# Score products of a gated recurrence: full 128 x 128 matmuls against column groups of 32 and 64 in heads 1 to 7

## The chip, the core and the metric

The kernel runs on one core of one Trainium2 chip. The metric is the device time of one execution in microseconds (us), and less is better. Five engines run beside each other and wait for each other through semaphores: TensorE (PE; its weight loads are shown apart as PEld), VectorE (DVE), ScalarE (ACT), GpSimd (POOL) and SyncE (SP), which here only issues DMAs.

## What is computed

The reference is a trunk of two layers on 256 tokens of 1024 features in fp32: a gated linear recurrence (HGRN2, 8 heads of 128 features), a SwiGLU, block attention, a second SwiGLU, with a norm ahead of each. The change is in the recurrence:

```python
q, fz, inp, og = jnp.split(proj, [...], axis=-1)     # proj = h @ w_in
q = jax.nn.silu(q)
f = lbf + (1.0 - lbf) * jax.nn.sigmoid(fz)
k = 1.0 - f
...
cum = jnp.cumsum(gb, axis=2)                         # gb = log f, in chunks of 64 tokens
diff = cum[:, :, :, None, :] - cum[:, :, None, :, :]
decay = jnp.exp(jnp.where(causal[:, :, None], diff, -jnp.inf))
scores = jnp.einsum('bhtn,bhsn,bhtsn->bhts', qb, kb, decay)
o = (jnp.einsum('bhts,bhsd->bhtd', scores, ib)
     + jnp.einsum('bhtn,bhnd->bhtd', qb * jnp.exp(cum), state))
```

So a token t sees a token s at or before it, and the product of their query and key is weighted, feature by feature, with the product of all forget gates f from s + 1 to t.

## The kernel before

**Main stream.** TensorE works through one long list of weight pieces. For each head the function `feature_major` computes three projections (forget, query, output gate) from 8 pieces of 128 x 128 weights each. `mm_w` issues three matmuls of 256 columns for each piece: weights and activations are split into a high and a low part, and high x high, low x high and high x low are added. The high part of a weight (`whi`) is made by ACT (L471), the low part (`wlo`) by DVE (L473), in blocks of 1024 columns, from weights that SP's queue loads. That is 72 main matmuls a head, into banks of the PSUM ring `psB`.

**The scores of a head.** `Core.scores` does not run over chunks. It splits the 256 x 256 score matrix by the distance of the two tokens: level m (2, 4, 8, 16, 32, 64, and 128 as the last one) holds the pairs whose tokens lie in the two halves of one block of 2m tokens. For each level `Core.step` has DVE and ACT make keys and queries that carry the gates' products up to the middle of the block, so that one matmul of keys by queries gives the level's scores. One such matmul of 128 keys by 128 queries gives the pairs between all blocks, of which only those within a block are wanted. They lie near the diagonal: `take` (DVE, `copy_predicated` with a mask) copies them into the score matrix `pm`; for levels 32 and 64 and the last one `far` (ACT) copies the square parts. Only these products are fp32 and not split, and each is issued by the hardware program as two matmuls with a weight load each. Per head there are:

- `s0`: two products for level 2 (rows named `psA<-mov,k`), into bank `b0`
- `level` for m = 4, 8 and 16 into a second bank, and for m = 32 and 64 into `b3` (rows `psA<-q,k`; level 64 is `psA<-q,bt`, since its keys lie inside the tile `bt`)
- the sums of the diagonal, with a matrix of ones as the weights (`psA<-q,ones`), into `b0`
- the last level, `kk` x `q128`, into `b3` (`psA<-bt,k`)
- `values`, the score matrix by the values `ii`, into `b4` (`psA<-bt,ii`)

These four banks are new for each head from the PSUM ring `psA`, which has four.

**Order.** The program's order is set while the kernel is written out, by the class `Order`. It keeps a planned clock for each engine. Main matmuls are issued in their list's order, and each moves the plan's time on. All other work is queued with a planned cost and a due time (`od.op(engine, cost, ...)`); after every main matmul or two `pump` emits what is ready in the plan. An operation of TensorE is put between main matmuls as soon as its operands are planned to have been ready for 1500 ns. `ct(n)`, the planned cost of an fp32 product, is 216 ns for 128 queries. The planned costs move nothing on the chip by themselves, but they decide where in TensorE's list a product stands, and in what order DVE, ACT and POOL take their work.

Of the kernel before, what the change touches and what calls it, by code (L numbers as in the profile page):

```python
# [335 lines left out]
def hybrid_trunk(ctx: ExitStack, tc: tile.TileContext, wts, xT, par, gfin, tab, onehot, masks, out):  # L336
# [218 lines left out]
    def mm(o, a, b, start=False, stop=False):  # L555
        T.matmul(o, a, b, start=start, stop=stop, skip_group_check=True)  # L556
# [311 lines left out]
    def normed(h, b, due):  # L868
# [4 lines left out]
              alloc=[t], due=due)  # L873
        return t, lambda: t.tile

    class Core:


# [61 lines left out]
        def step(self, m, due):  # L940
            Q, K, tot = self.Q, self.K, self.tot[m]
            if m < 64:
                k, kn = self.k1 if m == 1 else K[2], K[2]
                n = P // m
                bc = lambda z: cut(tot, z, (n + 1 - 2 * z, 2), (2, n // 2), (0, m))
                if m == 1:

                    q, pair = self.mov, self.tot[2]
                    od.op("V", cv(P), lambda: V.tensor_tensor(
                        cut(q, 0, (385, 2), (64, 2), (2, 32)), cut(q, P, (192, 2), (1, 2), (2, 32)),  # L950
                        cut(tot, 0, (P + 1, 2), (2, 2), (4, 32)), op=OP.mult), reads=[q, tot], writes=[q], due=due)
                    od.op("V", cv(P), lambda: V.tensor_tensor(
                        cut(q, 1, (383, 2), (64, 2), (2, 32)), cut(q, 192, (64, 2), (1, 2), (2, 32)),
                        cut(pair, 0, (64, 2), (1, 2), (2, 32)), op=OP.mult), reads=[q, pair], writes=[q], due=due)
                    od.op("V", cv(P), lambda: V.tensor_tensor(
                        first(kn, 1), k[:, :P].rearrange("p (a t) -> p a t", a=2), second(tot, 1), op=OP.mult),
                        reads=[k, tot], writes=[kn], due=due)
                    return
                elif m == 2:
                    q, qn = self.mov, Q[4]  # L960
                    of = lambda z: cut(q, 64 * z, (448 - P * z, 2), (2, 32), (1, 2))
                else:
                    q, qn = Q[m], Q[2 * m]
                    of = lambda z: (first, second)[z](q, m)
                od.op("V", cv(P), lambda: V.tensor_tensor(second(qn, m), of(1), bc(0), op=OP.mult), reads=[q, tot],
                      alloc=[qn], due=due)
                o = od.op("A", ca(P), lambda: A.activation(first(qn, m), of(0), AF.Copy), reads=[q], writes=[qn],
                          due=due + .1)
                o.deps.append(qn.writers[0])

                kk, kn = self.kk, K[2 * m]
                if m == 2:
                    od.op("V", cv(P), lambda: V.tensor_tensor(first(kk, m), first(k, m), bc(1), op=OP.mult),
                          reads=[k, tot], alloc=[kk], due=due)
                    o = od.op("A", ca(P), lambda: A.activation(second(kk, m), second(k, m), AF.Copy), reads=[k],
                              writes=[kk], due=due + .1)
                    o.deps.append(kk.writers[0])
                else:
                    od.op("V", cv(P), lambda: V.tensor_tensor(first(kk, m), first(kk, m), bc(1), op=OP.mult),
                          reads=[kk, tot], writes=[kk], due=due)  # L980
                od.op("A", ca(P), lambda: A.activation(
                    joint(kn, 2 * m).rearrange("p (b z i) -> p b z i", z=2, i=2 * m),
                    cut(kk, 0, (4 * m, 32 // m), (P + 2 * m, 2), (1, 2 * m)), AF.Copy), reads=[kk], alloc=[kn], due=due + .2)
                return
            self.q128 = q = new("q128", [P, P], 2)
            Q, k = Q[64], self.kk

            def last():
                A.activation(q[:, :64], Q[:, P:192], AF.Copy, scale=tot[:, 3:4])
                A.activation(q[:, 64:], Q[:, 192:], AF.Copy)  # L990
                A.activation(k[:, :64], k[:, :64], AF.Copy, scale=tot[:, 1:2])
            od.op("A", 3 * ca(64) + 186, last, reads=[Q, k, tot], writes=[k], alloc=[q], due=due)

        def scores(self, due):
            h, Q, K, mov = self.h, self.Q, self.K, self.mov
            pm = pms[h % 2]
            moff = {m: 2 * P + P * i for i, m in enumerate(LEVELS)}

            def take(m, src):
                d = ((2 * m, 64 // m), (1, m))  # L1000
                V.copy_predicated(cut(pm, m, (S - m, 2), *d), cut(mk, moff[m], (64, 2), (m, 64 // m), (1, m)), src)

            def level(b, c, m):

                mm(b[:, c:c + P], joint(K[m], m), second(Q[m], m), start=True, stop=True)

            b0 = bank("A")
            ev = self.even

            def s0():  # L1010


                for a, (c, to) in enumerate(((64, 64), (S, 192))):
                    mm(b0[:, to:to + P].rearrange("p (y x) -> p y x", y=2), K[2][:, a * P:a * P + P],
                       cut(mov, c, (P, 2), (1, 64)), start=True, stop=True)
            od.op("T", 2 * ct(P), s0, reads=[K[2], mov], alloc=[b0], due=due)

            def s0e():
                v = b0[:, :384].rearrange("p (a y x) -> p a y x", a=2, y=3)[:, :, 0:3:2]
                V.copy_predicated(pm[:, 0:3:2].rearrange("p a (x z) -> p a z x", z=2),  # L1020
                                  mk[:, :2 * P].rearrange("p (a z x) -> p a z x", a=2, z=2), v)
            od.op("V", cv(P), lambda: take(2, cut(b0, 64, (192, 2), (2, 32), (1, 2))), reads=[b0, mk], writes=[pm], due=due)
            b, o1 = bank("A"), None
            for i, m in enumerate((4, 8, 16)):
                o = od.op("T", ct(P), lambda m=m, i=i: level(b, P * i, m), reads=[K[m], Q[m]], due=due,
                          **(dict(writes=[b]) if i else dict(alloc=[b])))
                o.deps += [o1] if i else []
                o1 = o
                od.op("V", cv(P), lambda m=m, i=i: take(m, cut(b, P * i, (64, 2), (m, 64 // m), (1, m))), reads=[b, mk],
                      writes=[pm], due=due)  # L1030
            od.op("T", ct(P), lambda: mm(cut(b0, 0, (320, 2), (1, 64)), ones128, ev[:, EVEN].rearrange("p (a x) -> p a x", a=2),
                                         start=True, stop=True), reads=[ev], writes=[b0], due=due)
            od.op("V", cv(S), s0e, reads=[b0, mk], writes=[pm], due=due)
            b3, o1 = bank("A"), None
            for i, m in enumerate((32, 64)):
                o = od.op("T", ct(P), lambda m=m, i=i: level(b3, P * i, m), reads=[K[m], Q[m]], due=due,
                          **(dict(writes=[b3]) if i else dict(alloc=[b3])))
                o.deps += [o1] if i else []
                o1 = o
            o3 = od.op("T", ct(P), lambda: mm(b3[:, 2 * P:3 * P], self.kk[:, :P], self.q128.tile, start=True, stop=True),  # L1040
                       reads=[self.kk, self.q128], writes=[b3], due=due)
            o3.deps.append(o1)

            def far():
                for r, n, a, t, c in ((0, 32, 0, 32, 0), (64, 32, 0, 96, 32), (32, 32, 2, 0, 64), (96, 32, 2, 64, 96),
                                      (0, 64, 0, 64, P), (64, 64, 2, 0, 192)):
                    A.activation(pm[r:r + n, a, t:t + n], b3[r:r + n, c:c + n], AF.Copy)
                A.activation(pm[:, 1, :], b3[:, 2 * P:3 * P], AF.Copy)
            od.op("A", 1500, far, reads=[b3], writes=[pm], due=due)

            b4 = bank("A")
            hs = slice(h * P, h * P + P)

            def values():
                mm(b4[:, :S], ii[:, 0, hs], pm[:, 0:2, :].rearrange("p a t -> p (a t)"), start=True)
                mm(b4[:, P:S], ii[:, 1, hs], pm[:, 2, :], stop=True)
            od.op("T", ct(S) + ct(P), values, reads=[ii, pm], alloc=[b4], due=due)
            self.b4 = b4
# [22 lines left out]
    for h in range(NH):  # L1081
# [6 lines left out]
        if h == 0:  # L1088
            for k in range(KT):
                x0[k].free()  # L1090
    for k in range(KT):
        xs[k].free()
    sto.finish("A", 40)
# [577 lines left out]
```

## Time and profile before

| | |
|---|---|
| runs of the kernel | median 604.89 us of 3 (604.63 to 607.67) |
| the profiled execution | 605.56 us |
| its span, first to last instruction | 603.8 us |
| clock that TensorE was granted | 0.998 of full speed |
| TensorE's weight loads, whole program | 566.9 us busy |
| DMA | 120.85 MB, mean 200 GB/s |

The span is what the trace's rows add up to; the 1.8 us around it are start and end of the execution. In rows of groups, `out<-in` are the tiles by their names, `128*128 128x256` the rows and columns of the weights and the shape of what is streamed, `x64` the number of instructions, then their busy time in all and the mean duration of one. TensorE's matmuls are pipelined: their durations overlap, and how much of its time one takes is seen from when the next one starts. Timelines give start and duration in us from the span's beginning.

The recurrence of the eight heads lies between some 36 and 126 us, with 11 us a head.

### The profile page before, as it was taken

To read this page: it belongs to the slowest core of one execution; us is meant where nothing else is said; L and a number is where in the kernel's file an instruction comes from. 1 tells how busy PE (TensorE), PEld (TensorE's weight loads), DVE (VectorE), ACT (ScalarE), POOL (GpSimd) and SP (SyncE) were. 2 spreads that over 40 slices of the span, in tenths; PEclk is the share of its full clock that TensorE was granted. 3 is DMA by queue.
4 is the path that set the end of the run, shared out by engine and by line. 5 is a ranking of instruction groups with operands and counts; after the bars stand their busy time and mean duration, and the time that the engine had idled before them with its cause. 6 is when DMAs were issued, how large, how long until landed. Compare 5 with 4: busy or idle time off the path is not lost.

```text
span 603.8 us, 12020 instructions
## 1 busy us (share of the span) xinstructions
PE 595.6 (99%) x4508; PEld 566.9 (94%) x4508; DVE 514.7 (85%) x938; ACT 414.5 (69%) x816; POOL 62.4 (10%) x109
## 2 busy tenths in 40 slices
PE   9999999999999999999999999999999999999995
PEld 7899999999999999999988899999999999999984
DVE  6799988869797889889999678876789798889985
ACT  7698998957676476666838576655676576667763
POOL 0034141100101111110000100000100000000003
PEclk9999999999999999999999999999999999999999
DMA  8845542554847989889645764437565677778601
GB/s 315 327 167 190 178 166 95 170 170 161 261 152 158 270 232 254 258 249 263 236 164 170 254 208 153 163 140 236 177 213 164 223 239 232 227 215 256 196 34 69
DMA packets 35558, 120.85 MB, mean 200 GB/s; under 512 B 4812, under 2 KB 6348, under 8 KB 35501
## 3 DMA queue, kind: packets, MB, share of 16 engines
q1 hardware_dynamic: 31484, 109.05, 52.0%
q0 software_dynamic: 3056, 10.29, 10.1%
q10 hardware_dynamic: 960, 0.76, 0.4%
q8 instruction: 35, 0.57, 0.4%
q14 instruction: 23, 0.18, 0.1%
HBM read 118.71 MB, written 1.38 MB: 199 GB/s over the span
## 4 chain that ended last, share of the span: by engine, by line
PE 97%; DVE 1%; issue 0%; ACT 0%; POOL 0%; DVEq 0%; POOLq 0%; ACTq 0%
PE psB L556 50%; PE psA L556 47%; DVE ii L1318 1%; PE psB L1477 0%; PE psB L1381 0%; PE psA L1525 0%; DVE raw L1556 0%; DVE wlo L473 0%; PE psA L735 0%; PE psB L735 0%; DVE raw L1595 0%; DVE hl L1267 0%; DVE u L1257 0%; ACT fa L1579 0%; POOL ident masks.py:199 0%
## 5 line engine op out<-in xcount | busy, mean ns | idle before, releaser
L473 DVE TENSOR_TENSOR wlo<-raw,whi 128x1024 fp32r<-128x1024 f32 (+1 forms) x186 | 220.2, 1200 | 26.7 <-ACT whi L471 26.2
L471 ACT ACTIVATE whi<-raw 128x1024 fp32r<-128x1024 f32 (+1 forms) x185 | 188.2, 1038 | 43.7 <-PE psA L556 24.4
L556 PE MATMUL psB<-xh,whi 128*128 128x256 f32 x608 | 171.7, 286 | 0.0
L556 PE MATMUL psB<-xh,wlo 128*128 128x256 f32 x608 | 166.8, 278 | 0.0
L556 PE MATMUL psB<-xl,whi 128*128 128x256 f32 x608 | 162.3, 278 | 0.0
L556 PE MATMUL psA<-xh,whi 128*128 128x256 f32 x544 | 151.2, 281 | 0.0
L556 PE MATMUL psA<-xh,wlo 128*128 128x256 f32 x544 | 148.8, 277 | 0.0
L556 PE MATMUL psA<-xl,whi 128*128 128x256 f32 x544 | 143.7, 277 | 0.0
L556 PEld LDWEIGHTS psB<-xh,wlo 128*128 128x128 f32 x608 | 114.5, 188 | 0.7
L556 PEld LDWEIGHTS psB<-xh,whi 128*128 128x128 f32 x608 | 114.4, 188 | 0.7
L556 PEld LDWEIGHTS psB<-xl,whi 128*128 128x128 f32 x608 | 111.6, 189 | 0.0
L556 PEld LDWEIGHTS psA<-xh,wlo 128*128 128x128 f32 x544 | 102.4, 188 | 0.7
L556 PEld LDWEIGHTS psA<-xh,whi 128*128 128x128 f32 x544 | 102.2, 188 | 0.9
L556 PEld LDWEIGHTS psA<-xl,whi 128*128 128x128 f32 x544 | 99.2, 188 | 0.0
L1245 ACT ACTIVATE sgq<-sgq 128x256 f32<-128x256 f32 x44 | 18.2, 415 | 24.8 <-DVE sgq L1243 24.8
L556 PE MATMUL psB<-whi,hl 128*128 128x512 f32 (+1 forms) x91 | 35.1, 386 | 0.0
L556 PE MATMUL psB<-wlo,hh 128*128 128x512 f32 (+1 forms) x91 | 34.9, 383 | 0.0
L556 PE MATMUL psB<-whi,hh 128*128 128x512 f32 (+1 forms) x91 | 34.6, 380 | 0.1
L512 POOL DMA_DIRECT2D raw<-in_w_dram x13 | 11.7, 897 | 191.6 <-DVE wsum L504 177.8
L556 PE MATMUL psA<-whi,hh 128*128 128x512 f32 (+1 forms) x75 | 28.4, 379 | 0.3 <-DVE ii L1318 0.3
L556 PE MATMUL psA<-whi,hl 128*128 128x512 f32 (+1 forms) x75 | 28.6, 381 | 0.0
L556 PE MATMUL psA<-wlo,hh 128*128 128x512 f32 (+1 forms) x75 | 28.5, 380 | 0.0
(244 smaller groups left out, 980.7 us busy)
## 6 DMA issues: line engine op xcount, KB each, us to landing
raw<-in_w_dram SPq DMA_DIRECT2D x178, 512.0 KB, 4.3
bt<-in_w_dram SPq DMA_DIRECT2D x15, 512.0 KB, 5.1
raw<-in_w_dram POOLq DMA_DIRECT2D x13, 512.0 KB, 5.7
ii<-in_w_dram SPq DMA_DIRECT2D x9, 512.0 KB, 4.3
hT<-in_x_dram SPq DMA_DIRECT2D x8, 128.0 KB, 5.1
raw<-in_w_dram SPq DMA_DIRECT2D x4, 256.0 KB, 3.9
bt<-scr POOLq DMA_DIRECT2D x16, 64.0 KB, 6.6
bt<-in_w_dram POOLq DMA_DIRECT2D x2, 512.0 KB, 6.3
```

The costliest lines, as they stand in the source:

```text
L471: oa = od.op("A", ca(n), lambda h=h, r=src, o=o, n=n: A.activation(h[:, :n], r[:, o:o + n], AF.Copy), reads=[src], alloc=[h], due=due)
L473: ov = od.op("V", cv(n), lambda h=h, lo=lo, r=src, o=o, n=n: V.tensor_tensor(lo[:, :n], r[:, o:o + n], h[:, :n].bitcast(FT), op=OP.subtrac ...
L512: od.op("G", 1000, lambda: nc.gpsimd.dma_start(b.tile, wts[c0 // CHUNK], accum_op=OP.add), writes=[b], nbytes=2 * 524288, due=due + 1)
L556: T.matmul(o, a, b, start=start, stop=stop, skip_group_check=True)
L1245: od.op("A", ca(S), lambda: A.activation(s.tile, s.tile, AF.Silu), reads=[s], writes=[s], due=due)
L1318: V.scalar_tensor_tensor(at(), m[:, :], c[:, tt:tt + 1], at(), op0=OP.mult, op1=OP.add)
```

## The change

For heads 1 to 7, each of the score products named above, but for the last level's, is computed in pieces that hold the wanted blocks. The 128 keys of a product are cut into 4 groups of 32 weight columns, and each group is multiplied by the 32 queries that belong to it, and placed by `tile_position` in a column group of the array of its own, with its output in 32 partitions of the bank. Level 64 has two groups of 64 keys with 64 queries. What lies outside these blocks isn't computed; the masks and square copies don't use it. Head 0 still computes full products, which writes all of the banks once, and it takes the four banks of `psA` for good: `score_bank` hands heads 1 to 7 the same bank for the same use. The planned cost of a changed product is 80 ns instead of 216. The first product of the keys of a head (`kn` for m = 1) gets a dependency on the first writer of that tile.

```diff
+    def score_bank(h, i):
+        if h == 0:
+            b = bank("A", held=True)
+            r = Ring(lambda: b.tile, 1)
+            user = Buf(r)
+            user.readers, user.writers = b.readers, b.writers
+            r.past.append(user)
+            scored[i] = b, r, user
+            return b
+        b, r, _ = scored[i]
+        u = r.new()
+        scored[i] = b, r, u
+        return u
...
                         first(kn, 1), k[:, :P].rearrange("p (a t) -> p a t", a=2), second(tot, 1), op=OP.mult),
-                        reads=[k, tot], writes=[kn], due=due)
+                        reads=[k, tot], writes=[kn], due=due).deps.append(kn.writers[0])
...
+            cost = ct(P) if h == 0 else 80
+
             def level(b, c, m):
 
-                mm(b[:, c:c + P], joint(K[m], m), second(Q[m], m), start=True, stop=True)
-
-            b0 = bank("A")
+                keys, d = joint(K[m], m), ((m, 16 // m), (1, m)) if m <= 16 else ()
+                if h == 0:
+                    mm(b[:, c:c + P], keys, second(Q[m], m), start=True, stop=True)
+                elif m == 64:
+                    for z in range(2):
+                        small(b[64 * z:64 * z + 64, c + 64 * z:c + 64 * z + 64], keys, Q[m][:, 64 + 64 * z:P + 64 * z], z, 64)
+                else:
+                    for g in range(4):
+                        z, j, p = g % 2, g // 2, b[32 * g:32 * g + 32, :]
+                        if m == 32:
+                            at, to = m + 96 * z + 64 * j, c + 64 * z + 32 * j
+                            small(p[:, to:to + m], keys, Q[m][:, at:at + m], g, m)
+                        else:
+                            small(cut(p, c + 16 * g, (64, 2), *d), keys, cut(Q[m], m + 32 * g, (P - m, 2), (2 * m, 16 // m), (1, m)),
+                                  g, 32)
+
+            def small(o, keys, moving, g, n):
+                T.matmul(o, keys[:, n * g:n * g + n], moving, start=True, stop=True, skip_group_check=True,
+                         tile_position=(0, n * g))
+
+            b0 = score_bank(h, 0)
...
+                    if h:
+                        for g in range(4):
+                            small(cut(b0[32 * g:32 * g + 32, :], to + 16 * g, (64, 2), (1, 16)), K[2][:, a * P:a * P + P],
+                                  cut(mov, c + 16 * g, (P, 2), (1, 16)), g, 32)
+                        continue
...
-            od.op("T", 2 * ct(P), s0, reads=[K[2], mov], alloc=[b0], due=due)
+            od.op("T", 2 * cost, s0, reads=[K[2], mov], alloc=[b0], due=due)
...
+                for g in range(4):
+                    small(cut(b0[32 * g:32 * g + 32, :], 16 * g, (320, 2), (1, 16)), ones128,
+                          cut(ev, EVEN.start + 16 * g, (64, 2), (1, 16)), g, 32)
```

With another planned cost, products and main matmuls interleave in another way. Two places on TensorE show it. The first is around the `values` of head 0 (`psA<-bt,ii`); the `q` rows are head 1's levels, the `mov` row is level 2 of head 2. Before:

```order
L556 MATMUL psB<-xl_486,whi 128x256
L556 MATMUL psA<-q_839,k_826 128x128
L556 MATMUL psB<-xh_474,whi 128x256
L556 MATMUL psB<-xh_474,wlo 128x256
L556 MATMUL psB<-xl_496,whi 128x256
L556 MATMUL psA<-bt,ii 128x256
L556 MATMUL psA<-bt,ii 128x128
L556 MATMUL psA<-q_884,bt 128x128
L556 MATMUL psA<-mov,k_835 128x128 x2
L556 MATMUL psB<-xh_519,whi 128x256
```

and after the change, where a row of L1041 is a run of narrow matmuls:

```order
L556 MATMUL psB<-xl_419,whi 128x256
L1041 MATMUL psA<-mov,k_846 32x2x16 x8
L556 MATMUL psA<-bt,ii 128x256
L556 MATMUL psA<-bt,ii 128x128
L1041 MATMUL psA<-q_874,k_867 32x32 x4
L556 MATMUL psB<-xh_424,whi 128x256
L556 MATMUL psB<-xh_424,wlo 128x256
L556 MATMUL psB<-xl_437,whi 128x256
L556 MATMUL psB<-xh_426,whi 128x256
L556 MATMUL psB<-xh_426,wlo 128x256
L556 MATMUL psB<-xl_439,whi 128x256
L1041 MATMUL psA<-q_843,k_833 32x2x16 x4
```

Level 2 of head 2 has moved ahead of `values`, level 32 of head 1 (`32x32`) stands right behind it, and full matmuls lie between the three runs of narrow ones. The second place is TensorE at head 1's first level. Before, the last level's product of head 0 (`psA<-bt,k`) and level 8 of head 1 stand together:

```order
L556 MATMUL psB<-xl_496,whi 128x256
L556 MATMUL psA<-bt,k_572 128x128
L556 MATMUL psA<-q_802,k_788 128x128
L556 MATMUL psB<-xh_519,whi 128x256
L556 MATMUL psB<-xh_519,wlo 128x256
```

and after:

```order
L556 MATMUL psB<-xl_541,whi 128x256
L556 MATMUL psA<-bt,k_572 128x128
L1041 MATMUL psA<-q_766,k_760 32x2x16 x4
L1041 MATMUL psA<-q_692,ones_109 32x2x16 x4
L556 MATMUL psB<-xh_400,whi 128x256
```

Here level 4 and the diagonal's sums of head 1 have come together behind that product, so that two changed products share one place. In all, the 49 rows of L1041 stand in 44 places: between two places lies at least one full matmul, or, in one case, a change from groups of 32 to groups of 64.

More of the change, by code (lines that the diff above doesn't have):

```diff
@@ L874, in normed @@
         return t, lambda: t.tile
+    scored = {}
+    def score_bank(h, i):
[11 more added lines that the diff above has]
+        return u
     class Core:
@@ L1022, in scores @@
             od.op("V", cv(P), lambda: take(2, cut(b0, 64, (192, 2), (2, 32), (1, 2))), reads=[b0, mk], writes=[pm], due=due)
-            b, o1 = bank("A"), None
+            b, o1 = score_bank(h, 1), None
             for i, m in enumerate((4, 8, 16)):
-                o = od.op("T", ct(P), lambda m=m, i=i: level(b, P * i, m), reads=[K[m], Q[m]], due=due,
+                o = od.op("T", cost, lambda m=m, i=i: level(b, P * i, m), reads=[K[m], Q[m]], due=due,
                           **(dict(writes=[b]) if i else dict(alloc=[b])))
@@ L1030, in scores, with sums @@
                       writes=[pm], due=due)
-            od.op("T", ct(P), lambda: mm(cut(b0, 0, (320, 2), (1, 64)), ones128, ev[:, EVEN].rearrange("p (a x) -> p a x", a=2),
-                                         start=True, stop=True), reads=[ev], writes=[b0], due=due)
+            def sums():
+                if h == 0:
+                    mm(cut(b0, 0, (320, 2), (1, 64)), ones128, ev[:, EVEN].rearrange("p (a x) -> p a x", a=2),
+                       start=True, stop=True)
+                    return
+                for g in range(4):
+                    small(cut(b0[32 * g:32 * g + 32, :], 16 * g, (320, 2), (1, 16)), ones128,
+                          cut(ev, EVEN.start + 16 * g, (64, 2), (1, 16)), g, 32)
+            od.op("T", cost, sums, reads=[ev], writes=[b0], due=due)
             od.op("V", cv(S), s0e, reads=[b0, mk], writes=[pm], due=due)
-            b3, o1 = bank("A"), None
+            b3, o1 = score_bank(h, 2), None
             for i, m in enumerate((32, 64)):
-                o = od.op("T", ct(P), lambda m=m, i=i: level(b3, P * i, m), reads=[K[m], Q[m]], due=due,
+                o = od.op("T", cost, lambda m=m, i=i: level(b3, P * i, m), reads=[K[m], Q[m]], due=due,
                           **(dict(writes=[b3]) if i else dict(alloc=[b3])))
@@ L1049, in scores @@
             od.op("A", 1500, far, reads=[b3], writes=[pm], due=due)
-            b4 = bank("A")
+            b4 = score_bank(h, 3)
             hs = slice(h * P, h * P + P)
@@ L1090, in hybrid_trunk @@
                 x0[k].free()
+    for b, _, u in scored.values():
+        b.readers += u.readers + u.writers
+        b.held = False
     for k in range(KT):
```

## The prediction

> **What bounds the kernel now.** I read the page first: the busy shares, then the chain that ended last.
>
> ```profile
> span 603.8 us, 12020 instructions
> PE 595.6 (99%) x4508; PEld 566.9 (94%) x4508; DVE 514.7 (85%) x938; ACT 414.5 (69%) x816; POOL 62.4 (10%) x109
> PE 97%; DVE 1%; issue 0%; ACT 0%; POOL 0%; DVEq 0%; POOLq 0%; ACTq 0%
> ```
>
> The chain is TensorE (PE) for 97% of the span. A busy PE can still hide waiting, so the next view is that of the waits, for PE alone and the whole program. It has two rows:
>
> ```profile
> PE psA L556 <- POOL ident masks.py:199: 1.4, 1, 1.4
> PE psA L556 <- DVE ii L1318: 0.3, 1, 0.3
> ```
>
> PE waits once at the start and once in the last layer, never in the recurrence. So each microsecond that the change adds to or takes from PE's stream there should reach the end, as long as the other engines keep up. For that I read the table of windows over heads 1 to 7 (44 to 124 us; columns: stretch, length, then the busy time of PE, PEld, DVE, ACT, POOL, granted clock, DMA share, GB/s):
>
> ```profile
> 44.00:124.00 80.00, 80.00 (x686) 79.63 (x684) 72.95 (x186) 70.52 (x233) 20.20 (x48) 1.00 0.47 164
> ```
>
> PE is full and its clock is whole. VectorE (DVE) is busy for 72.95 of 80 us: about 7 us is the most that PE could gain here before DVE were the bound. If PE gets longer, nobody else is touched.
>
> **What is removed.** The groups of instructions, kept apart by shape, show the score products as fp32 matmuls of 128 x 128 with 128 queries. Each product is issued as two matmuls (two halves), each with its own weight load.
>
> ```profile
> L556 PE MATMUL psA<-q,k 128*128 128x128 f32 x64 | 11.8, 274 | 0.0
> L556 PE MATMUL psA<-mov,k 128*128 128x128 f32 x32 | 4.9, 274 | 0.0
> L556 PE MATMUL psA<-q,ones 128*128 128x128 f32 x16 | 3.1, 273 | 0.0
> L556 PE MATMUL psA<-q,bt 128*128 128x128 f32 x16 | 3.1, 273 | 0.0
> ```
>
> The counts are for eight heads: 128 halves, 64 products, 8 a head (levels 4, 8, 16, 32; two for level 2; the sums; level 64). Heads 1 to 7 lose 56 products. The 274 ns are a pipelined duration, not a price; the price is read from the chain, where a product stands between pieces of the main stream:
>
> ```profile
> 47.48 0.22 PE psA L556 x2
> 47.70 1.42 PE psB L556 x12
> ```
>
> A product takes 0.22 us of PE's time, 0.11 us a half; a main matmul takes 1.42/12 = 0.118 us. Removed: 56 x 0.22 = **12.3 us**.
>
> **What the narrow products cost in themselves.** Each of 49 products becomes 4 narrow ones (32 weight columns, 32 queries), hence 8 halves; each of the 7 of level 64 becomes 2 of 64, hence 4 halves. No row of this trace has a load of 32 columns or two column groups at once, so I bound it. What paces a half is seen at 151 us, where a half streams a single column:
>
> ```profile
> 151.66 0.53 PEld L556 LDWEIGHTS psB<-ones,sqacc 128*128 128x128 f32 x4
> 152.21 0.18 PEld L556 LDWEIGHTS psB<-ohr,tbh 33*128 33x128 f32 x1
> 152.67 0.18 PEld L556 LDWEIGHTS psB<-ohr,tbl 33*128 33x128 f32 x1
> 153.00 0.19 PEld L556 LDWEIGHTS psA<-xh,whi 128*128 128x128 f32 x1
> 153.11 0.19 PEld L556 LDWEIGHTS psA<-xh,wlo 128*128 128x128 f32 x1
> ```
>
> Four loads last 0.53 us, one lasts 0.19, so they start (0.53 - 0.19)/3 = 0.11 us apart though almost nothing is streamed. The load of 128 columns alone sets the pace, and it is as long as the stream of 128 queries. Scaled to a quarter, a narrow half has 0.0275 us of load and 0.0275 us of stream. Upper end: the load doesn't scale, 8 x 0.11 = 0.88 us a product. One after another at a quarter each: 8 x 0.0275 = 0.22 us, exactly what is removed, so that narrowing alone gains nothing. Lower end: the four groups run side by side, 2 x 0.0275 = 0.055 us. I assume that the two halves of a group, which share its columns, follow each other, and that a neighbour's load runs beside them; I take 4 x 0.031 = 0.125 us a product, a little over one half for each group, and keep 0.055 and 0.22 for the range. Level 64 lies between the same ends (2 x 0.055 to 4 x 0.055) and is taken alike. Added: 56 x 0.125 = **7.0 us**.
>
> The Trainium skill ("TensorE: Matmul & The Clock Gate", Part 3) says that matmuls in different tiles of the array start about 4 ns apart and overlap; an estimate by it is 0.055 + 3 x 0.004 = 0.07 us a product, and the forecast below would be 611.7. The same page (Part 1) has start-to-start never under about 25 ns however short the matmul; by that, 8 x 0.025 = 0.20 us and 619.0. No run here shows either for column groups.
>
> **What it costs to change the shape.** This is the term that decides. The array is used in parts at one place only: the two bias products with 33 rows, among full matmuls. PE's timeline there:
>
> ```profile
> 151.42 0.52 PE L556 MATMUL psA<-xl,whi 128*128 128x256 f32 x3
> 151.78 0.50 PE L556 MATMUL psB<-ones,sqacc 128*128 128x1 f32 x4
> 152.21 0.44 PE L556 MATMUL psB<-ohr,tbh 33*128 33x384 f32 x1
> 152.49 0.34 PE L556 MATMUL psB<-ohr,tbl 33*128 33x384 f32 x1
> 152.67 0.29 PE L556 MATMUL psB<-ohr,tbh 33*128 33x256 f32 x1
> 152.79 0.28 PE L556 MATMUL psB<-ohr,tbl 33*128 33x256 f32 x1
> 153.00 0.39 PE L556 MATMUL psA<-xh,whi 128*128 128x256 f32 x1
> 153.22 0.28 PE L556 MATMUL psA<-xh,wlo 128*128 128x256 f32 x1
> 153.34 0.28 PE L556 MATMUL psA<-xh,whi 128*128 128x256 f32 x1
> ```
>
> Going in: the last full load starts at 151.66 + 0.34 = 152.00, the next is due at 152.11 and starts at 152.21, 0.10 us late. Coming out: in the plain stream a load starts together with the matmul before it (153.11 lies 0.11 after 153.00, and then 0.12 apart). Here the load for xh,whi does not start at 152.79 but at 153.00, as though the array had to empty first, and its matmul then has to wait for its own load: from 152.79 to 153.22 two matmuls of 256 columns take 0.43 us instead of 2 x 0.118, which is 0.19 us lost. The waits view has no wait for data here. So one visit to another shape costs 0.10 + 0.19 = 0.29, say 0.30 us. In the main stream a visit also exposes its first narrow load: 0.03 us if it scales, 0.11 if not. I take **0.33 us a visit**, with 0.30 and 0.41 as ends.
>
> That these rows show rows cut and the change cuts columns is the weak point of the argument. The Trainium skill ("TensorEngine Tiling (Array Packing)", Tiling Modes, Key Properties) makes no such difference: a change of the tiling mode drains TensorE, a change of tile within a mode does not. By that rule the price holds for column groups too; the trace agrees for rows, with its 0.30 us.
>
> How many visits: PE's order shows the 49 rows of narrow products (7 of level 2 as x8) in 44 places between full matmuls, since only a few share a place and full matmuls stand between the others (the two places shown with the change are of this kind). 44 x 0.33 = **14.5 us**. The old products cost nothing there: the chain has the main stream resume after 0.22 us.
>
> **What costs nothing.** The narrow products write fixed banks that head 0 takes; before, each head took the four banks of the same ring in turn, so a bank is reused one head later either way. The added dependency makes the first key product of a head wait for a ScalarE copy that is planned ahead of it; queued behind it on DVE stand the weight splits that PE needs. Its row:
>
> ```profile
> L955 DVE TENSOR_TENSOR k<-k,ff 128x128 f32<-128x128 f32 x8 | 2.3, 287 | 0.0
> ```
>
> It has waited for nothing so far; if it did for its own length, 7 x 0.29 = 2 us of DVE would go, inside the 7 us that DVE is idle. DVE, ACT and POOL instructions are the same ones in a shifted order, SP's queue is unchanged. PE gets longer, so this cover only grows.
>
> **Sum.** Against the profiled execution's own 605.56 us (span 603.8; the median of the runs is 604.89, 0.1% below): - 12.3 + 7.0 + 14.5 = +9.2, so **614.8 us**. Its own ends: 44 x 0.30 + 56 x 0.055 - 12.3 = +4.0, 609.6; 44 x 0.41 + 56 x 0.22 - 12.3 = +18.0, 623.6.
>
> **Rivals.**
> 1. Column groups need no emptying, and the groups overlap. Then 7.0 - 12.3 = -5.3: 600.3 us, faster; 596.4 with 0.055 a product, if DVE's 7 us allowed it. For it: the bias products cut rows, and their visit ends in a different kind of full matmul only once. Against it: nothing in their rows ties the late loads to rows. It decides at (12.3 - 7.0)/44 = 0.12 us a visit: below that the change gains, above it loses. The first page named stands on this side as far as it speaks of overlap.
> 2. No emptying, but the halves run one after another: 0.22 for 0.22, 605.6 us, no change.
> 3. The groups are narrow in the program only, and each load takes its full 0.11 us: 49 x 0.88 + 7 x 0.44 = 46.2; 639.5 without visits and 654 with them. This is also the case in which the change does not do what it says. Against it: the program issues the matmuls with 32 partitions out.
>
> **Chances.** Forecast 0.61, rival 1 0.23, rival 2 0.11, rival 3 0.05. The emptying is seen for rows, so I hold it likely, not sure, for columns. Rival 1 must lie in the range, and rival 3 and the thin ends may stay out: 599 to 622; the forecast's own range is 609.6 to 622. More than 0.5% (3 us, about what a measurement of this kernel can tell from no change) faster: 0.23; within: 0.11; slower: 0.66.
>
> **What would show it.** In the profile after, around a group of narrow matmuls: the load of the next full weights starts 0.2 us after the last narrow matmul (right) or together with it (rival 1). The start of the first narrow matmul to that of the last, by 8 halves: 0.016 us a half is my figure, 0.007 side by side, 0.0275 in turn, 0.11 rival 3. The stretch from 44 us to the end of head 7 should be 9 us longer, with DVE's busy time unchanged at about 73 us and PE waiting for nobody. I am wrong if the full stream resumes at its 0.118 us pace right behind a group, or if PE waits for DVE's splits.

## The result, and the profile after

The changed kernel takes **614.63 us** (median of 4 runs, 613.68 to 615.59) against 605.15 us for the kernel before, run beside it: a ratio of 1.0148, with a 95% interval of 1.0115 to 1.0182. The profiled execution took 613.68 us, 8.1 us more than the profiled execution before. The forecast was 614.8 us.

The page after, by the same lines as before (busy time and share by engine, then the chain that ended last):

```profile
span 611.9 us, 12616 instructions
PE 601.9 (98%) x4816; PEld 564.9 (92%) x4816; DVE 515.0 (84%) x938; ACT 414.6 (68%) x816; POOL 64.4 (11%) x109
PE 97%; DVE 2%; ACT 0%; issue 0%; POOL 0%; DVEq 0%; POOLq 0%; ACTq 0%
```

PE is still the chain; DVE's and ACT's busy times are what they were. New is DVE's 2% (1% before) and, in the view of the waits, the first of PE's rows:

```profile
PE psA L556 <- ACT xh L678: 1.7, 1, 1.7
```

The other two are those of before.

The table of windows for heads 1 to 7 (44 to 124 us, columns as before) has PE full again, while DVE has less to do per microsecond, since the same heads now last longer:

```profile
44.00:124.00 80.00, 80.00 (x931) 72.90 (x930) 68.36 (x176) 65.81 (x219) 21.62 (x48) 1.00 0.46 146
```

**Where the time came from.** The two timelines of PE are held against each other at the same main matmuls: the last one of the output projection that follows the heads (`psB<-xl,whi`), and the one right behind it (`psA<-xh,whi`), the first of the SwiGLU. Before:

```profile
140.35 0.28 PE L556 MATMUL psB<-xl,whi 128*128 128x256 f32 x1
140.47 0.28 PE L556 MATMUL psA<-xh,whi 128*128 128x256 f32 x1
```

and after:

```profile
145.96 0.28 PE L556 MATMUL psB<-xl,whi 128*128 128x256 f32 x1
147.98 0.38 PE L556 MATMUL psA<-xh,whi 128*128 128x256 f32 x1 [1.74 <-ACT xh L678]
```

Up to the end of the output projection the change has cost 145.96 - 140.35 = 5.6 us; in the next step it costs (147.98 - 140.47) - 5.6 = 1.9 us more, by a wait; from there to the end of the span (8.1 us) another 0.6 us in small pieces. So the 8.1 us are two things: visits to the narrow shape, and one wait behind the last head.

**A visit, close up.** PE's timeline around one narrow product (L1041, 8 halves) in head 1, and the weight loads at its end:

```profile
59.48 0.28 PE L556 MATMUL psB<-xh,wlo 128*128 128x256 f32 x1
59.59 0.28 PE L556 MATMUL psB<-xl,whi 128*128 128x256 f32 x1
59.80 0.27 PE L1041 MATMUL psA<-q,k 128*32 128x32 f32 x8
60.00 0.38 PE L556 MATMUL psB<-xh,whi 128*128 128x256 f32 x1
60.22 0.28 PE L556 MATMUL psB<-xh,wlo 128*128 128x256 f32 x1
...
59.80 0.16 PEld L1041 LDWEIGHTS psA<-q,k 128*32 128x32 f32 x8
60.00 0.19 PEld L556 LDWEIGHTS psB<-xh,whi 128*128 128x128 f32 x1
```

In the plain stream a matmul starts 0.118 us after the other. Here the first narrow one starts 0.21 us after the full one before it (0.09 late); the next full load starts at 60.00, at the same time as its matmul and not a matmul ahead of it, and the matmul behind that comes 0.22 us later (0.10 late). From 59.59 to 60.22 two full matmuls take 0.63 us instead of 0.236: the visit costs 0.39 us. The same place with two products, levels 4 and the sums:

```profile
65.82 0.28 PE L556 MATMUL psB<-xl,whi 128*128 128x256 f32 x1
66.03 0.27 PE L1041 MATMUL psA<-q,k 128*32 128x32 f32 x8
66.11 0.25 PE L1041 MATMUL psA<-q,ones 128*32 128x32 f32 x8
...
66.52 0.28 PE L556 MATMUL psB<-xh,wlo 128*128 128x256 f32 x1
```

From 65.82 to 66.52 that is 0.70 - 0.236 = 0.46 us. So the second product adds some 0.065 us (0.063 and a little more in the trace's nanoseconds), and a visit without any product would cost 0.39 - 0.064 = **0.325 us**.

The trace has 43 such places (one of the 44 goes over from groups of 32 to groups of 64 in passing): 25 of one product at 0.389, 11 of two at 0.455, 6 of level 64 at 0.456 (medians), and that one at 0.718, together 18.2 us. Less the 12.3 us removed this is 5.9 us, where the timelines show 5.6; the first experiment says where the rest is.

### The profile page after: what moved, and what is told of

It is laid out like the page before. It is cut to its first block, busy times and chain, and to the rows that moved or that the text cites. A ratio compares the mean times of both kernels' runs of the same rounds, so it can differ in the third digit from the quotient of the medians.

```text
span 611.9 us, 12616 instructions
## 1 busy us (share of the span) xinstructions
PE 601.9 (98%) x4816; PEld 564.9 (92%) x4816; DVE 515.0 (84%) x938; ACT 414.6 (68%) x816; POOL 64.4 (11%) x109
## 4 chain that ended last, share of the span: by engine, by line
PE 97%; DVE 2%; ACT 0%; issue 0%; POOL 0%; DVEq 0%; POOLq 0%; ACTq 0%
PE psB L556 50%; PE psA L556 44%; PE psA L1041 2%; DVE ii L1371 1%; PE psB L1530 0%; DVE wlo L473 0%; PE psA L1578 0%; PE psB L1434 0%; DVE raw L1609 0%; DVE yt L746 0%; ACT whi L471 0%; DVE hT L748 0%; ACT xh L678 0%; PE psB L735 0%; PE psA L735 0%
## 5 line engine op out<-in xcount | busy, mean ns | idle before, releaser
L1298 ACT ACTIVATE sgq<-sgq 128x256 f32<-128x256 f32 x44 | 18.2, 415 | 28.6 <-DVE sgq L1296 28.6
```

The costliest lines, as they stand in the source:

```text
L1298: od.op("A", ca(S), lambda: A.activation(s.tile, s.tile, AF.Silu), reads=[s], writes=[s], due=due)
```

## The experiments

In all of them what is computed remains the same, except where it is said. Ratios are to the kernel before, run beside it on the same chip. The runs of the kernel before alone lie between 604 and 608 or 609 us, so differences of 1 to 2 us between two medians are read from the traces, not from the times.

### The order without the narrow products

The changed kernel, with full products in heads 1 to 7 as well, in `level`, `s0` and the sums:

```diff
-                if h == 0:
+                if True:
                     mm(b[:, c:c + P], keys, second(Q[m], m), start=True, stop=True)
```

> The changed kernel with its banks, its added dependency and its order (planned cost 80), but with the full 128 x 128 products of before in all heads. If the visits to another shape are the whole price, the head stage (44 us to the end of head 7) costs what it cost before, and the time is 604.5 to 605.7. If the order that comes from the planned cost of 80 makes the new wait at 140 us (ACT's split for the first matmuls after the output projection), that wait of some 1.7 to 2.2 us is here too, and the time is 606.5 to 607.5. If the order itself, not the shape, lost the 5.4 us in the heads, the time is 610 or more.

606.98 us, ratio 1.0022 (1.0007 to 1.0037). PE's waits:

```profile
PE psA L556 <- ACT xh L678: 1.7, 1, 1.7
```

The wait is here without a single narrow matmul, and the stretch of the heads is as long as before (from the 285th to the 810th of the matmuls with a split weight, which is from some 53 to 134 us in the kernel before, 80.8 us; before 80.7, after the change 86.1). The last matmul of the output projection starts here at:

```profile
140.02 0.28 PE L556 MATMUL psB<-xl,whi 128*128 128x256 f32 x1
```

That is 0.3 us earlier than before, so the other order in itself saves a little. Against this run, which has the order of the changed kernel, the narrow products cost 145.96 - 140.02 = 5.94 us, as much as the sum of the places says. So the loss in the heads belongs to the narrow products, and the wait belongs to something else in the change.

### The planned cost

```diff
-            cost = ct(P) if h == 0 else 80
+            cost = ct(P) if h == 0 else 390
```

and 455 for `s0`.

> The changed kernel with a planned cost for each narrow product that is near what a visit takes in its trace (390 ns; 455 for level 2) in place of 80; the products themselves as in the changed kernel. My theory (a visit costs 0.325 us, a product 0.064): still 42 to 46 visits, so the head stage is 5 to 6 us longer than before; and if the wait at 140 us comes from a plan that runs ahead of the chip, it goes, and the time is 612 to 613. Rival: the wait comes from the longer visits of head 7 themselves, or from the banks, and stays: 614 to 615.

612.08 us, ratio 1.0099 (1.0067 to 1.0130): as expected, and the wait at the end of the heads is gone. But the places are 35, where 42 to 46 were expected (the plan now puts more products together), and PE has new waits of 2.0 us in the heads, for DVE's and ACT's keys and queries. That the wait went doesn't show that a plan ahead of the chip had made it; the full products with the planned cost of before settle that, below.

### Fewer places

All narrow products of a head in two places, or in one, by one operation of the plan for each place:

```diff
+                for visit in VISITS:                 # ((2, 1, 4, 8), (16, 32, 64)); or all seven in one
+                    o = od.op("T", 330 + 64 * len(visit), lambda visit=visit: [parts[p][0]() for p in visit],
+                              reads=reads, due=due, ...)
```

> The same narrow products, but grouped: in each of heads 1 to 7 level 2, the sums, levels 4 and 8 stand together in one place, levels 16, 32 and 64 in another; 14 places with full matmuls between them instead of 44. My theory (0.325 us a visit, 0.064 a product, 0.135 for going from groups of 32 to groups of 64): 14 x 0.325 + 56 x 0.064 + 7 x 0.135 - 12.3 = -3.2 against before, so 602, and 604 if the wait at 140 us stays. Rival: the price is one for each product (a change of operands or of partitions), not for each place; then 49 x 0.29 is still there and the time stays at 613 to 615.

> The same narrow products, all of a head in one place: 7 places. My theory: 7 x (0.325 + 0.135) + 56 x 0.064 - 12.3 = -5.5 against before, so 599.7 (602 if the wait at 140 us stays); visit by visit each costs some 0.9 us. Rival 1, a price for each product: 613 to 615. Rival 2: PE is no longer the bound, since all of a head's copies of DVE and ACT come at once and late (DVE has some 7 us of idle time in 80 in heads 1 to 7); then the waits view shows PE waiting for DVE or ACT in the recurrence, and the time is 602 or more.

Two places took 609.24 us, ratio 1.0048 (1.0027 to 1.0069); one place 608.32 us, ratio 1.0021 (1.0004 to 1.0039). On PE each does what the price by places says. A place with five products (level 2, sums, 4, 8), in the kernel with two places:

```profile
56.45 0.28 PE L556 MATMUL psB<-xl,whi 128*128 128x256 f32 x1
56.66 0.33 PE L1043 MATMUL psA<-mov,k 128*32 128x32 f32 x16
56.81 0.25 PE L1043 MATMUL psA<-q,ones 128*32 128x32 f32 x8
56.87 0.35 PE L1043 MATMUL psA<-q,k 128*32 128x32 f32 x16
...
57.37 0.28 PE L556 MATMUL psB<-xh,wlo 128*128 128x256 f32 x1
```

From 56.45 to 57.37 it is 0.92 - 0.236 = 0.68 us for five products, where one alone takes 0.39. The price is one for the place: five products in five places would take 1.95 us. The second place (16, 32, 64) takes 0.72, so 14 places cost 9.8 us instead of 18.2; a single place for all costs 1.08, so 7 places 7.6 us. That is 2.5 and 4.7 us less than the removed 12.3 us.

Neither gain arrives, because PE now waits. In the kernel with one place:

```profile
PE psA L556 <- ACT bt L1122: 3.3, 3, 2.0
...
PE psA L1043 <- ACT q L986: 0.6, 1, 0.6
```

The first row is the `values` product waiting for the last of the square copies of `far`. This kernel's chain can be followed back to 103 us, and from there to 130 us no piece of it is PE's: it goes through DVE's splits and masked copies (`bt L1020`), ACT's copies and back. The second rival of this expectation holds: with one place a head PE is no longer the bound there.

With two places the time fits neither the expectation (602 or 604) nor its rival (613 to 615). The loss lies behind the heads: a wait of 1.9 us for the split of head 7's output, and again the 1.7 us for `xh L678`. Right behind each of them the granted clock was 0.50 for 3.4 us, from 132.6 and from 142.9 us on, as the table of windows shows for a part of the first:

```profile
133.00:136.00 3.00, 3.00 (x16) 3.00 (x15) 1.42 (x2) 0.00 (x0) 0.00 (x0) 0.50 0.64 228
```

The twelve main matmuls from 132.55 us on took 2.96 us instead of 1.42, and those that took 9.5 us before, from 140.5 to 150.0 us, took 11.2 us here. Besides, both profiles lost 2.1 us to the slow pace of which the last section tells.

### All queries for each group

Each column group multiplies all 128 queries, as the full product does:

```diff
-                            small(p[:, to:to + m], keys, Q[m][:, at:at + m], g, m)
+                            small(b[n * g:n * g + n, c:c + P], keys, second(Q[m], m), g, n)
```

and alike in level 2 and the sums.

> The changed kernel with its order and its visits, but each column group multiplies all 128 queries (4 x 32 or 2 x 64 weight columns, 128 queries each) in place of its own 32 or 64. If the groups run side by side, a product of 8 halves takes some 2 x 0.11 = 0.22 us, the toll stays, and the time is 0.16 x 56 = 9 us over the changed kernel: 622 to 625. If they share the stream of queries and run in turn, a product takes 4 x 0.22 = 0.88 us, and the time is 650 to 660.

624.53 us, ratio 1.0301 (1.0260 to 1.0342), as expected for groups side by side. The same place as in the close-up:

```profile
59.33 0.28 PE L556 MATMUL psB<-xl,whi 128*128 128x256 f32 x1
59.54 0.43 PE L1033 MATMUL psA<-q,k 128*32 128x128 f32 x8
...
60.12 0.28 PE L556 MATMUL psB<-xh,wlo 128*128 128x256 f32 x1
```

0.79 - 0.236 = 0.55 us instead of 0.39; a second product in the place adds 0.218 us. Eight halves of 128 queries take as long as two full halves: the four groups run side by side, and the toll (0.55 - 0.22 = 0.33) is untouched by what is streamed.

### One or two places with their true price

One place planned at 1083 ns; the same with `values` put later; two places planned at 700 ns:

```diff
-                    o = od.op("T", 330 + 64 * len(visit), ...
+                    o = od.op("T", 390 + 693 * (len(visit) > 4), ...        # one place: 1083 (two places: 700 here)
...
-            od.op("T", ct(S) + ct(P), values, ...)
+            od.op("T", ct(S) + ct(P), values, ..., early=2500.0 if 0 < h < NH - 1 else None)
```

> One place for all narrow products of a head, as in the run with 7 places, but planned at 1083 ns, which is what such a place was seen to take. By the sum of the places 7 x 1.08 - 12.3 = -4.7 us against before. If a plan that knows the price takes PE's waits for ACT's square copies (3.3 us) and in the tail away, the time is 600.5 to 602.5 where before is 605.5. Rival: the waits come from the chain of DVE's masked copies and ACT's square copies, which start only when all products are done; then the waits view keeps 2 us or more of them, and the time is 604 to 607.

> As the one before, and in heads 1 to 6 the values product is put behind main matmuls until its operands have been ready for 2500 ns in the plan, in place of 1500. If waiting for ACT's square copies is what keeps one place a head from its -4.7 us, these waits are gone from the waits view (under 0.5 us), and the time is 600.5 to 602.5 where before is 605.5. Rival: the later values make head 7's tail or the next head late, and the loss moves there: 604 to 607.

> Two places a head, each planned at the 700 ns that were seen (0.684 and 0.716). By the sum of the places 7 x 1.40 - 12.3 = -2.5 us against before. If the 8 us that were lost between 133 and 150 us with two places came from the order that the too low planned cost made (weight splits ahead of the sums' chain on ACT and DVE), they are gone: 602.5 to 603.5 where before is 605.5. Rival: they come from narrow products as such, and stay: 607 or more.

The first took 612.36 us, ratio 1.0093 (1.0062 to 1.0124), a miss for the first expectation: `values` still waits 3.8 us for `far`, and the wait for `xh L678` is there again. It lies above the rival's 604 to 607 too; here as well the granted clock was 0.50 for 3.4 us, from 99.8 us on, behind one of the waits of `values`. With `values` later, 609.69 us, ratio 1.0044 (1.0020 to 1.0067): the wait of `values` fell to 1.0 us, but others of 0.7 to 1.7 us appeared, for DVE and ACT, in other places, so the loss moved as the rival had it, and was larger than its 604 to 607. Two places with their price took 605.27 us, ratio 0.9983 (0.9963 to 1.0004), a smaller gain than the 2 to 3 us expected; PE doesn't wait for `xh L678`, and its clock is whole behind the heads. Its waits in the heads and right behind them:

```profile
PE psB L556 <- ACT bt L957: 0.5, 1, 0.5
PE psA L1043 <- ACT q L986: 0.4, 1, 0.4
PE psA L556 <- ACT bt L1122: 0.3, 1, 0.3
PE psA L1043 <- DVE bt L1020: 0.2, 1, 0.2
```

These 1.4 us come off the 2.5, and what is left is not more than a measurement of this kernel can tell.

### Only one narrow shape

Level 64 as four groups of 32 keys, each with its 64 queries, in the same order as the run before:

```diff
-                    for z in range(2):
-                        small(b[64 * z:64 * z + 64, c + 64 * z:c + 64 * z + 64], keys, Q[m][:, 64 + 64 * z:P + 64 * z], z, 64)
+                    for g in range(4):
+                        z = g // 2
+                        small(b[32 * g:32 * g + 32, c + 64 * z:c + 64 * z + 64], keys, Q[m][:, 64 + 64 * z:P + 64 * z], g, 32)
```

> The kernel with two places a head and a planned cost of 700, in the same order, but level 64 as four groups of 32 keys with 64 queries each in place of two groups of 64. If going from groups of 32 to groups of 64 has a price of its own, the second place (0.716 us, of which level 64 adds 0.263 to a place with two products) falls to 0.453 + 0.11 = 0.56, where 0.11 lies between the 0.064 of 32 queries and the 0.218 of 128; over 7 heads 1.1 us, so 604.2 where two places took 605.3. If only the longer stream or the wider load made level 64 dear, the place stays at 0.70 or more and the time at 605.3.

> As the run with level 64 in four groups of 32, but the second place planned at 560 ns, what it should take, in place of 700, so that the order is another one. By the sum of the places 7 x (0.684 + 0.56) - 12.3 = -3.6 us; if the plan's nearness to the chip is what keeps PE from waiting, the time is 603 to 604 where before is 606; if the order that a planner happens to give decides, waits of 1 to 4 us come back and the time is 605 to 609.

A second place with groups of 64 (L1043, two places planned at 700):

```profile
88.65 0.28 PE L556 MATMUL psB<-xl,whi 128*128 128x256 f32 x1
88.85 0.33 PE L1043 MATMUL psA<-q,k 128*32 128x32 f32 x16
89.11 0.34 PE L1043 MATMUL psA<-q,bt 128*64 128x64 f32 x4
...
89.60 0.28 PE L556 MATMUL psB<-xh,wlo 128*128 128x256 f32 x1
```

and with groups of 32 alone:

```profile
88.81 0.28 PE L556 MATMUL psB<-xl,whi 128*128 128x256 f32 x1
89.02 0.33 PE L1044 MATMUL psA<-q,k 128*32 128x32 f32 x16
89.16 0.30 PE L1044 MATMUL psA<-q,bt 128*32 128x64 f32 x8
...
89.62 0.28 PE L556 MATMUL psB<-xh,wlo 128*128 128x256 f32 x1
```

0.95 against 0.81 us: going from groups of 32 to groups of 64 costs some 0.14 us of its own, as expected. But the time is 605.00 us, ratio 0.9988 (0.9969 to 1.0007): both profiles have a span of 602.3 us. PE's waits in the heads and behind them rose from 1.4 to 1.9 us, which is half of the 1.0 us that was saved; the other half I can't name. With the places planned at 684 and 560 ns the time is 605.77 us, ratio 1.0008 (0.9992 to 1.0025), the second case of its expectation: between the same two matmuls as above it gained 2.8 us on the kernel before (77.9 us), and the wait of 1.7 us for `xh L678` came back.

### What makes the wait behind the heads

Full products everywhere and the planned cost of before (`cost = ct(P)`); once with banks and dependency, once without the dependency:

```diff
-                        reads=[k, tot], writes=[kn], due=due).deps.append(kn.writers[0])
+                        reads=[k, tot], writes=[kn], due=due)
```

> Full products everywhere and the planned cost of before (216), with the fixed banks and the added dependency of the changed kernel: these two alone. My theory: the wait of 1.7 us at 140 us comes from the order that the planned cost of 80 makes, so it is gone here, and the time is that of before within 0.3 us. Rival: the dependency or the banks make it; then ACT's split for the first matmuls after the output projection is in the waits view with 1.7 us, and the time is 0.6 to 1.5 us over before.

> Full products everywhere, the planned cost of before (216) and the fixed banks, but without the added dependency: the run with both lost 1.7 us to the wait at 140 us (and 2.3 us in the first SwiGLU). With the banks alone the order of all engines is that of before; so if the order makes the wait it is gone, and the time is that of before within 0.3%. If holding the four banks makes it, the wait for ACT's split (1.7 us) stays with the order of before. If the 2.3 us in the first SwiGLU came with the banks, they stay too: 1.003 to 1.004.

With both it took 609.55 us, ratio 1.0057 (1.0033 to 1.0080), and the row of the wait for `xh L678` is there again, with 1.7 us. So my theory that the planned cost of 80 made it has fallen. (2.1 us more of this profile were lost in the first SwiGLU, for which see the last section.) With the banks alone it took 605.41 us, ratio 1.0008 (0.9991 to 1.0024), and no wait for `xh L678` is in the view. My expectation said that with the banks alone the order was that of before on all engines. It isn't: the traces have several hundred rows of PE and over a hundred of DVE in another place. It is so at the place in question on DVE.

What the wait consists of is seen in the timeline of DVE there (`wlo` is the low part of a weight block, `yt` and `hT` are the sum of trunk and output projection, from which ACT's `xh L678` makes what PE waits for). Before:

```profile
135.94 1.23 DVE L473 TENSOR_TENSOR wlo<-raw,whi 128x1024 fp32r<-128x1024 f32 x1 [1.74 <-ACT whi L471]
137.08 0.68 DVE L746 TENSOR_TENSOR yt<-psB,rrow 128x512 f32<-128x512 f32 x1
137.80 0.69 DVE L748 TENSOR_TENSOR hT<-yt,hT 128x512 f32<-128x512 f32 x1
```

and after:

```profile
144.37 1.22 DVE L473 TENSOR_TENSOR wlo<-raw,whi 128x1024 fp32r<-128x1024 f32 x1 [1.98 <-ACT whi L471]
145.51 1.28 DVE L746 TENSOR_TENSOR yt<-psB,rrow 128x512 f32<-128x512 f32 x2
146.71 1.28 DVE L748 TENSOR_TENSOR hT<-yt,hT 128x512 f32<-128x512 f32 x2
```

Counted from the last matmul of the output projection, `yt` started 3.3 us ahead of it before, and 0.5 us ahead of it after. It stands behind a weight split that waits for ACT's `whi`, and that in turn for PE: the end of the chain of waits after shows it (DVE's and ACT's pieces between two of PE).

```profile
142.09 1.15 PE psB L556 x9
...
143.27 1.07 ACT whi L471
...
144.37 1.22 DVE wlo L473
145.59 1.20 DVE yt L746 x2
146.79 0.61 DVE hT L748
...
147.42 0.52 ACT xh L678
...
147.98 4.04 PE psA L556 x32
```

In the program's order for DVE, the kernels with this wait (the changed one and seven of the experiments) all have `yt` twice, `hT` twice, `xl`, `yt`; those without it (four experiments) have `yt` twice, `hT` twice, `yt`, `xl`; the kernel before and the one with the banks alone have `yt`, `hT`, `yt`, then a split. No kernel is an exception, with full or narrow products, with planned costs of 80, 216, 390 and more. What it comes down to is one weight split: in the timelines of all eight kernels with the wait 49 splits `wlo` stand on DVE ahead of the first `yt`, in the six without it 48. The 49th needs a `whi` of ACT, which starts when PE's piece before it ends, at 142.09 + 1.15 = 143.24 us. The last matmul of the output projection starts 2.7 us later, but the pieces from there through `xh` take 4.7 us: the next matmul starts 2.0 us behind that last one, where before it was 0.12 us. The wait is a matter of this order. The dependency alone was not run; written out, it leaves the order of before on every engine as it was, so that at the planned cost of before only banks and dependency together bring the other order. Which decision of the planner does it stays open.

## Why the prediction was right, and where it was not

The time came within 0.2 us of the median, but by two errors that cancel, so that the nearness is luck.

- **What bounds the kernel.** Right for the heads: PE stayed full and paid for every visit. That nobody else would be touched was wrong: "PE waiting for nobody" failed with the one wait of 1.7 us behind the heads. I had named DVE's splits as what could prove me wrong, and one of them stands in that chain. But I had costed the added dependency, the banks and the shifted order at nothing, by DVE's idle time in the heads. The key product with the dependency (`k<-k,ff`) still waits for nothing, as I had it; what dependency and banks changed is the order. That cover says nothing on a short chain at the end of a stage, where the kernel before served PE in time.
- **The toll of a visit.** Right, and for the right reason: 0.33 us forecast from two products with 33 rows, 0.325 us measured for column groups. In the parts it differs: 0.09 going in (0.10 and the exposed load of 0.03 forecast), 0.23 coming out (0.19 forecast), and the full load starts 0.13 us after the last narrow matmul's start, not 0.2. The parts miss in opposite directions, so that the sum is nearer than they are. Places: 43 instead of 44. The Trainium skill ("TensorEngine Tiling (Array Packing)", Tiling Modes, Key Properties) has a drain for a change of mode and none for a change of tile; the runs agree: five products in a place pay once (0.68 us), and going from groups of 32 to groups of 64 pays again (0.14 us).
- **The narrow product.** The step that failed was "I take 4 x 0.031 = 0.125 us a product": it measured 0.064, at the side-by-side end of my range (0.055). The two halves of a group don't hold its neighbours up. So 7.0 us were 3.6 us, and a little more for level 64 (its place of one product takes 0.456 instead of 0.389 us). The run with all queries shows the same: 0.218 us for four groups of 128 queries. My estimate by the Trainium skill ("TensorE: Matmul & The Clock Gate", Part 3), 0.07 us, is close to what was measured; the smallest distance of 25 ns between starts in Part 1 of that page of the Trainium skill would have made 0.20 us, and doesn't hold across column groups, where eight halves take 64 ns.
- **What was removed.** 12.3 us: the visits' 18.2 us less this are 5.9, and the timelines show 5.6 (5.94 in the same order) where the forecast had 9.2.
- **The rivals.** Rival 1 was half right: the groups overlap as it said, but the emptying is there, and it decides: 0.325 us a visit lies far above the 0.12 us (with the true prices 0.19 us) below which the change would gain. Rivals 2 and 3 are out.

Sum of the profile: 5.6 us for visits and products, 1.9 us for the wait, 0.6 us behind it, 8.1 us. With the right price of a product my own sum would have been 5.8 us, 611.4, and the wait and the rest would have been missing.

Could grouping turn the change into a gain? On PE yes, by up to 4.7 us; in the time no version was faster than the kernel before by more than its measurement can tell. The nearest are two places a head (0.9983 and 0.9988, each with 1 in its interval).

## What to carry over

Small matmuls in column groups were cheap in themselves here (0.064 us a product), and changing the array's shape wasn't: count the places where the stream changes its shape, not the matmuls, and compare the toll with what a place saves (here 0.325 us a place against 0.22 - 0.064 = 0.16 us a product). Gathering the products into few places takes the toll away but makes their operands late, so that the bound moves to the engines that make and take them. And a change that leaves the sums of all engines as they were can still add a wait at the end of a stage: look at the short chains there, by their slack, before costing a new order at nothing.

## What was not expected of the hardware

The plain stream of main matmuls has two paces, and keeps one for a long time. Pieces of the chain in the first SwiGLU, of the kernel before and of the one with full products, banks and dependency; 51 matmuls each at the same point of the program:

```profile
232.79 6.16 PE psA L556 x51
```

```profile
235.22 6.36 PE psA L556 x51
```

The granted clock is 1.00 in both, PE waits for nobody, and yet a matmul takes 4 ns more (in the trace's nanoseconds, most starts lie 113 apart in the one and 117 or 118 in the other). From some 222 to 304 us this makes 2.1 us (84.1 us instead of 82.0). Four of the experiments' profiles had the slow pace there throughout (two places, one place, all queries, and this one), the others not or in part, and neither narrow products nor planned cost sets it apart. I had not reckoned with it, and what sets it is open; the runs of the kernel before, spread over some 4 us, are more than wide enough to hold it. The runs with one place a head fall in two groups, 606.1 to 606.5 us and 608.2 to 609.2 us; the one profile of them, with the slow pace, is of the upper group. That fits two paces of the same kernel, but isn't shown by it.

The other thing is that a wait can cost more than itself. Behind three waits of 1.7 to 2.0 us, in the kernel with two places and in that with one place at its true price, the granted clock was 0.50 for 3.4 us; behind the waits of 1.7 us for `xh L678` in the other profiles, and behind one of 2.0 us with one place a head, it stayed at 1.00. What decides between the two is not shown here.
